# A group norm's inverse roots on four columns, spread by DMA, and one form for all decay differences

## The chip, the cores and the metric

The kernel runs on one core of a Trainium2 chip. The metric is the time of one execution on the device in microseconds. Engines are named TensorE (PE in the profile, its weight loads PEld), VectorE (DVE), ScalarE (ACT), GpSimd (POOL) and SyncE (SP).

## What is computed

One layer of a hybrid decoder: a multi-scale causal pooling branch and a Mamba-2 branch, merged by gates, and then an MLP. 16 meta tokens stand ahead of 512 tokens of width 1024. The change touches the Mamba-2 branch alone. Cut to what matters:

```python
xbc = silu(causal_depthwise_conv(xbc, conv_w, conv_b))          # x, B, C of 8 groups with 4 heads each
a_cs = cumsum(dt * a)                                           # per head, in chunks of 128 tokens
diff = a_cs[:, :, :, None] - a_cs[:, :, None, :]                # decay differences
lmat = exp(where(mask, diff, -inf))
y_diag = einsum("bclsg,bclsgr,bcsgrp->bclgrp", cb, lmat, xdt)
y_off  = einsum("bclgn,bcgrpn,bclgr->bclgrp", cf, prev, exp(a_cs))
y = (y_diag + y_off + x * d_skip) * silu(z)
yg = y.reshape(bsz, seqlen, 8, 256)
yg = yg * rsqrt(mean(yg * yg, axis=-1, keepdims=True) + EPS)    # the scan's group norm
y_ssd = (yg.reshape(bsz, seqlen, 2048) * norm_w) @ w_ssd_out
```

## The kernel before

Channels lie on partitions, and the 512 tokens along the free axis. Each matmul in single precision is made of three in a faster format: `block` (L69, L70) loads a 128x1024 block of weights, ScalarE copies it to its high half `whi`, VectorE subtracts to get the low half `wlo`, and TensorE multiplies high by high, high by low and low by high. There are four buffers of `whi` and `wlo` and three of `raw`.

The scan is done for one group of four heads at a time: `ssd(g, cur)`, eight times. It is a generator, and `weave` alternates its steps with those of a second generator that gives TensorE work: `group_proj(g + 1)`, which projects the next group's B, C, x and z (tiles `bt`, `ct`, `xc`, `zt`; products `px` and `pz`), for g = 4 also `out_half` (products `pso`), and for g = 7 `out_part` (products `psp`). For g = 1, 2, 3 and 5 a gate (`pgp`) is projected as well, between the x and the z of the next group. The order in which each engine meets its instructions is then set by a scheduler that reorders them by its own estimates, so that TensorE's row of matmuls changes from one to another group.

The steps of `ssd` that matter here:

- `abc`, four heads by 512 tokens on all 128 partitions, is read from DRAM (`acs_d`) by a DMA of GpSimd, broadcast to the partitions. Two exponentials of it go to `eb` (L372).
- The tile is then turned in place into decay differences. Heads 0 and 1 go through ScalarE: Relu(bias - a), 8 instructions (L377). Heads 2 and 3 go through VectorE: min(a - bias, 0), 8 instructions (L380). The exponential of the first pair has the scale -1 (L382), that of the second pair 1 (L383).
- Transposes of `bt` and `xc` (`ptb`, `ptm`, `ptx`) give `xdt` and `xdd`; `pcb` is the product of B and C, which VectorE masks into `cbm` (L390) and multiplies into `abc` (L403). `pst` are the states of the chunks, carried on in `st` (L399 to L402).
- `po` (from `st`) and `py` (from `abc`) give `yt`, which VectorE finishes (L419 to L423).
- The group norm: the squares of `yt`, summed over the two halves, are split into `qh` and `ql`; a product with a matrix of ones (`png`, L432) puts the sum of each token on every partition. ScalarE takes the root of all 128 partitions by 512 tokens (L435, tile `rs`), VectorE the reciprocal in four pieces of 128 columns (L437) and the scaling of `yt` (L441); the result is split into `yh` on ScalarE (L444) and `yl` on VectorE (L445).

`rs` and `cbm` have the same tag and share one buffer; so have `eb` and `sqg`, the squares.

Of the kernel before, what the change touches and what calls it, by code (L numbers as in the profile page):

```python
# [9 lines left out]
F32 = mybir.dt.float32  # L10
F32R = mybir.dt.float32r
AF = mybir.ActivationFunctionType
ALU = mybir.AluOpType

P = 128
D = 1024
SEQ = 512
# [4 lines left out]
G = 8  # L22
R = 4
# [22 lines left out]
def kernel(ctx: ExitStack, tc, xT, x, w, vec, fnw, out):  # L46
    nc = tc.nc
    act, dve, pe, pool = nc.scalar, nc.vector, nc.tensor, nc.gpsimd
# [3 lines left out]
    dram = ctx.enter_context(tc.tile_pool(name="dram", bufs=1, space=bass.MemoryType.DRAM))  # L52
# [50 lines left out]
    eps = const.tile([P, 1], F32, name="eps")  # L103
# [7 lines left out]
    dtok = const.tile([P, 2, 4, HEADS], F32, name="dtok")  # L111
# [19 lines left out]
    def psum1(name):  # L131
        return psb.tile([P, 512], F32, tag="s", name=name)
# [41 lines left out]
    for k in range(NK):  # L174
        if k == 0:
# [4 lines left out]
                                 op0=ALU.mult, op1=ALU.subtract)  # L180
# [13 lines left out]
    def col_sums(name, qt, n2, tags, bufs=1):  # L194

        qh = n2.tile(list(qt.shape), F32R, tag=tags[0], name=f"qh{name}", bufs=bufs)
        ql = n2.tile(list(qt.shape), F32R, tag=tags[1], name=f"ql{name}", bufs=bufs)
        act.copy(qh, qt)
        dve.tensor_tensor(ql, qt, qh.bitcast(F32), op=ALU.subtract)
        return qh, ql  # L200


    qh, ql = col_sums("n1", q, pre, ("sq", "sq"), 2)
    for i in range(2):
        c = slice(i * HALF, (i + 1) * HALF)
        pn = psum1(f"pn1_{i}")
# [14 lines left out]
    for c in range(4):  # L221
        r = slice(c * H, (c + 1) * H)
# [20 lines left out]
    for c in (slice(0, P), slice(P, W)):  # L243
        n = c.stop - c.start
        dve.tensor_tensor_scan(acs[:, c], ones_f[:, :n], v[:, c], 0.0, op0=ALU.mult, op1=ALU.add)
    acs_d = dram.tile([H, SEQ], F32, name="acs_d")
    for c in range(4):
        nc.gpsimd.dma_start(acs_d[:, c * P : (c + 1) * P], acs[c * H : (c + 1) * H, :P])
    pt = psum1("pt_dt")
# [79 lines left out]
    def ssd(g, cur):  # L329
# [4 lines left out]
        ctok = lambda c: slice(c * P, (c + 1) * P)  # L334
        flat = lambda t: t.rearrange("p r d -> p (r d)")
        abc = gs.tile([P, R, SEQ], F32, tag="abc", name=f"abc{g}")
# [17 lines left out]
        for b in range(2):  # L354
            pt = psum1(f"ptx{g}_{b}")
            for c in range(2):
                for i in range(2):
                    o = c * 256 + i * P
# [14 lines left out]
        dm = abc.rearrange("p r (c l) -> p r c l", c=4)  # L373
        for r in range(R):
            for c in range(4):
                if r < 2:
                    act.activation(dm[:, r, c, :], dm[:, r, c, :], AF.Relu, scale=-1.0,  # L377
                                   bias=dtok[:, 1, c, R * g + r : R * g + r + 1])
                else:
                    dve.tensor_scalar(dm[:, r, c, :], dm[:, r, c, :], dtok[:, 1, c, R * g + r : R * g + r + 1],  # L380
                                      0.0, op0=ALU.subtract, op1=ALU.min)
        act.activation(abc[:, :2], abc[:, :2], AF.Exp, scale=-1.0)  # L382
        act.activation(abc[:, 2:], abc[:, 2:], AF.Exp)  # L383
        yield

        pc = psum1(f"pcb{g}")
# [20 lines left out]
        for i in range(2):  # L407
# [5 lines left out]
            for c in range(4):  # L413
                for j in range(2):
                    r = 2 * i + j
# [6 lines left out]
                                     op0=ALU.mult, op1=ALU.add)  # L422
# [6 lines left out]
        qh, ql = col_sums(f"g{g}", sq[:, 0, :], gs, ("qh", "ql"))  # L429
        yield  # L430
        pn = psum1(f"png{g}")
        pe.matmul(pn, ones_r, qh, start=True, stop=False)  # L432
        pe.matmul(pn, ones_r, ql, start=False, stop=True)
        rs = gs.tile([P, SEQ], F32, tag="cbm", name=f"rs{g}")
        act.activation(rs, pn, AF.Sqrt, bias=eps, scale=1.0 / 256)  # L435
        for c in range(4):
            dve.reciprocal(rs[:, ctok(c)], rs[:, ctok(c)])  # L437
        yield
        for i in range(2):
            y = yt[:, i, :]  # L440
# [34 lines left out]
    gs = gc_stack.enter_context(tc.tile_pool(name="gs", bufs=1, side="left", reuse_waits="tile"))  # L475
# [29 lines left out]
    for g in range(G):  # L505
        nxt = group_tiles(g + 1) if g + 1 < G else None
        fill = [group_proj(g + 1, nxt, GATE_AT.get(g))] if nxt else [out_part()]
        if g == 4:
            fill = [out_half()] + fill
        weave(ssd(g, cur), fill, 2 if g == 4 else 1)  # L510
        cur = nxt
# [75 lines left out]
    for d in range(NK):  # L587
        ps = psum2(f"pup{d}")[:, :SEQ]
        wh, wl = block()
        for n, k in enumerate(ks):  # L590
            c = slice(k * P, (k + 1) * P)
# [35 lines left out]
    for half in range(2):  # L627
# [5 lines left out]
        for kk in range(4):  # L633
            wh, wl = block()
            for k2 in range(2):
                k = 2 * kk + k2
                c = slice(k2 * 512, (k2 + 1) * 512)
# [4 lines left out]
        c = slice(half * 512, (half + 1) * 512)  # L642
        for t in range(4):
            dve.tensor_tensor(ht[:, t, c], ht[:, t, c], pv[t], op=ALU.add)
        for kk in range(4):
            k = 4 * half + kk
            pt = psum1(f"pth{k}")
            for t in range(4):
# [3 lines left out]
                                     op0=ALU.mult, op1=ALU.subtract)  # L652
        for t in range(4):
            j = hp_.tile([P, 512], F32, tag="junk", name=f"junk{half}_{t}", bufs=1)
# [171 lines left out]
    c = NC - 1  # L826
# [5 lines left out]
    for t in range(4):  # L832
        T, st = t // 2, slice((t % 2) * P, (t % 2 + 1) * P)
        n = 0
        for half in range(2):
            parts = [(0, 512)] if half == 0 or t < 3 else [(0, 256), (256, 256)]
            for a, m in parts:
# [4 lines left out]
                for k, seg in ((1, (A11, 3)[T]), (0, (A12, A22)[T])):  # L842
                    wh, wl = wq[k, half]
                    for p in range(2):
                        x0 = p * 512 + a
                        f = i == 0 and not (T == 0 and half == 0)
# [151 lines left out]
```

## Time and profile before

| | us |
|---|---|
| median of 3 runs | 1035.16 (1035.08 to 1035.29) |
| the profiled execution | 1035.26 |
| its span, from the first to the last instruction | 1033.5 |
| TensorE busy | 1019.6 |
| VectorE busy | 714.2 |
| ScalarE busy | 542.3 |
| GpSimd busy | 9.9 |

The granted clock of TensorE was 0.998 over the span. The time of an execution is 1.8 us more than the span, which begins at the first instruction and ends with the last. The scan (`ssd`) lies between about 69 and 485 us of the span; the pooling branch, the output projections and the MLP come after it. In a row of the profile, L437 is line 437 of the kernel before; `out<-in` names the tiles.

### The profile page before, as it was taken

Reading aid. Unit: us, or ns where it says so; the run is one execution under the profiler, and the core shown is the slowest. Engines: PE = TensorE matmul, PEld = TensorE weight load, DVE = VectorE, ACT = ScalarE, POOL = GpSimd, SP = SyncE. Lnnn points to the kernel's source line nnn. Section 1 sums busy time; section 2 is a strip of 40 time slices with the busy share of each in tenths; the row PEclk is TensorE's granted clock in tenths of the full one; section 3 lists DMA queues with packets and bytes.
Section 4 is the critical chain, followed back from the end, with each engine's and each line's share of the span. In section 5 each row is a group of like instructions: output and inputs, shape, how many; then the busy total and the mean of one; then the engine's idle time right before and its main releaser. Section 6 shows DMA issues by size and latency. Waiting matters only on the chain.

```text
span 1033.5 us, 13995 instructions
## 1 busy us (share of the span) xinstructions
PE 1019.6 (99%) x5700; PEld 880.2 (85%) x5700; DVE 714.2 (69%) x932; ACT 542.3 (52%) x706; POOL 9.9 (1%) x24
## 2 busy tenths in 40 slices
PE   7999999999999999999999999999999999999997
PEld 7889988898879898988998888878888888888886
DVE  7978787687636586878664345645686676776866
ACT  7675968586627349573443123344555354454444
POOL 0100000000000000000000000000000000000000
PEclk9999999999999999999999999999999999999999
DMA  6343041414332321413232323533324323334112
GB/s 229 110 140 103 21 164 37 148 47 137 102 112 73 103 101 41 146 59 111 77 107 95 102 81 102 204 126 122 99 82 123 103 81 122 102 102 123 42 41 82
DMA packets 29424, 106.01 MB, mean 103 GB/s; under 512 B 3312, under 2 KB 4272, under 8 KB 28336
## 3 DMA queue, kind: packets, MB, share of 16 engines
q1 hardware_dynamic: 26640, 93.14, 28.8%
q0 software_dynamic: 2000, 11.08, 2.9%
q8 instruction: 45, 0.74, 0.3%
q10 hardware_dynamic: 720, 0.91, 0.3%
q14 instruction: 19, 0.16, 0.0%
HBM read 102.95 MB, written 2.16 MB: 102 GB/s over the span
## 4 chain that ended last, share of the span: by engine, by line
PE 97%; DVE 1%; DMA 1%; ACT 0%; issue 0%; SPq 0%; ACTq 0%
PE px L138 6%; PE px L141 6%; PE px L139 6%; PE pf L86 6%; PE pf L87 6%; PE pf L88 6%; PE alpha L742 3%; PE alpha L743 3%; PE alpha L744 3%; PE pz L139 3%; PE pz L141 3%; PE pz L138 3%; PE py L416 2%; PE pso L86 2%; PE pp L141 2%; PE pp L139 2%
## 5 line engine op out<-in xcount | busy, mean ns | idle before, releaser
L69 ACT CAST whi<-raw 128x1024 fp32r<-128x1024 f32 (+2 forms) x141 | 145.4, 1037 | 274.3 <-PE pf L87 61.3
L70 DVE TENSOR_TENSOR wlo<-raw,whi 128x1024 fp32r<-128x1024 f32 (+2 forms) x141 | 169.8, 1206 | 151.5 <-ACT whi L69 151.5
L138 PE MATMUL px<-uh,whi 128*128 128x264 f32 (+1 forms) x448 | 121.0, 291 | 0.7 <-DVE ct L280 0.7
L139 PE MATMUL px<-ul,whi 128*128 128x264 f32 (+1 forms) x448 | 118.2, 284 | 0.0
L86 PE MATMUL pf<-vh,whi 128*128 128x512 f32 x256 | 99.7, 389 | 1.2 <-DVE vl L651 1.2
L87 PE MATMUL pf<-vl,whi 128*128 128x512 f32 x256 | 99.6, 389 | 0.0
L88 PE MATMUL pf<-vh,wlo 128*128 128x512 f32 x256 | 99.6, 389 | 0.0
L141 PE MATMUL px<-uh,wlo 128*128 128x264 f32 (+1 forms) x448 | 91.5, 285 | 0.0
L138 PEld LDWEIGHTS px<-uh,whi 128*128 128x128 f32 x448 | 84.6, 189 | 2.8 <-issue 2.6
L139 PEld LDWEIGHTS px<-ul,whi 128*128 128x128 f32 x448 | 84.4, 188 | 0.3
L141 PEld LDWEIGHTS px<-uh,wlo 128*128 128x128 f32 x448 | 69.4, 188 | 0.3 <-issue 0.3
L693 DVE TENSOR_TENSOR slo<-b,shi 128x1024 fp32r<-128x1024 f32 x35 | 42.7, 1220 | 31.6 <-ACT shi L692 31.6
L692 ACT CAST shi<-b 128x1024 fp32r<-128x1024 f32 x35 | 36.7, 1050 | 51.9 <-PE pf L87 36.5
L86 PEld LDWEIGHTS pf<-vh,whi 128*128 128x128 f32 x256 | 48.1, 188 | 11.5 <-DVE vl L651 1.5
L88 PEld LDWEIGHTS pf<-vh,wlo 128*128 128x128 f32 x256 | 48.0, 188 | 10.0
L87 PEld LDWEIGHTS pf<-vl,whi 128*128 128x128 f32 x256 | 48.1, 188 | 9.8
L742 PE MATMUL alpha<-shi,hh 128*128 128x512 f32 x140 | 54.6, 390 | 0.0
L743 PE MATMUL alpha<-slo,hh 128*128 128x512 f32 x140 | 54.5, 389 | 0.0
L744 PE MATMUL alpha<-shi,hl 128*128 128x512 f32 x140 | 54.5, 389 | 0.0
L754 DVE TENSOR_TENSOR ht<-ht,alpha 128x1024 f32<-128x1024 f32 x35 | 42.6, 1216 | 6.1 <-PE alpha L744 6.1
L139 PE MATMUL pz<-ul,whi 128*128 128x512 f32 x112 | 44.3, 395 | 0.0
L141 PE MATMUL pz<-uh,wlo 128*128 128x512 f32 x112 | 44.1, 394 | 0.0
(330 smaller groups left out, 2395.8 us busy)
## 6 DMA issues: line engine op xcount, KB each, us to landing
raw<-in_w SPq DMA_DIRECT2D x137, 512.0 KB, 3.6
b<-in_w SPq DMA_DIRECT2D x28, 512.0 KB, 3.5
abc<-acs_d POOLq DMA_DIRECT2D x8, 1024.0 KB, 7.2
xt<-in_xT SPq DMA_DIRECT2D x8, 264.0 KB, 6.2
ht<-in_x POOLq DMA_DIRECT2D x4, 512.0 KB, 5.0
w<-in_w SPq DMA_DIRECT2D x4, 512.0 KB, 3.5
out_dram<-out SPq DMA_DIRECT2D x4, 320.0 KB, 2.4
raw<-in_w SPq DMA_DIRECT2D x2, 384.0 KB, 5.5
```

What stands on the lines that cost most here:

```text
L69: act.copy(hi[:, c], raw[:, c])
L70: dve.tensor_tensor(lo[:, c], raw[:, c], hi[:, c].bitcast(F32), op=ALU.subtract)
L86: pe.matmul(ps, ah, bh, start=first, stop=False)
L87: pe.matmul(ps, ah, bl, start=False, stop=False)
L88: pe.matmul(ps, al, bh, start=False, stop=last)
L138: pe.matmul(o, wh, rhs[0][k][:, c], start=k == 0, stop=False)
L139: pe.matmul(o, wh, rhs[1][k][:, c], start=False, stop=False)
L141: pe.matmul(o, wl, rhs[0][k][:, c], start=False, stop=k == NK - 1)
L693: dve.tensor_tensor(lo, src, hi.bitcast(F32), op=ALU.subtract)
L742: pe.matmul(ps[t], a[0], wh[:, cs], start=f, stop=False, skip_group_check=True)
L743: pe.matmul(ps[t], a[0], wl[:, cs], start=False, stop=False, skip_group_check=True)
L744: pe.matmul(ps[t], a[1], wh[:, cs], start=False, stop=l, skip_group_check=True)
```

## The change

Two things are changed in `ssd`.

The root of the group norm is taken on one partition only: ScalarE reads the first partition of `png` and writes a row of 512 values. A DMA of GpSimd spreads this row over 128 partitions with four tokens on each (`rc`), VectorE takes the reciprocal of these 128x4 values, a second DMA writes them to a new tensor in DRAM (`rs_d`), and a third reads the 512 values back into all 128 partitions of `rs`. The scaling of `yt` reads `rs` as before.

The decay differences of all four heads go through ScalarE in the Relu form, 16 instructions, and one exponential with the scale -1 takes the whole tile of 128x2048.

```diff
@@ -244,6 +244,7 @@
     acs_d = dram.tile([H, SEQ], F32, name="acs_d")
+    rs_d = dram.tile([G, SEQ], F32, name="rs_d")
@@ -373,14 +374,9 @@
         dm = abc.rearrange("p r (c l) -> p r c l", c=4)
         for r in range(R):
             for c in range(4):
-                if r < 2:
-                    act.activation(dm[:, r, c, :], dm[:, r, c, :], AF.Relu, scale=-1.0,
-                                   bias=dtok[:, 1, c, R * g + r : R * g + r + 1])
-                else:
-                    dve.tensor_scalar(dm[:, r, c, :], dm[:, r, c, :], dtok[:, 1, c, R * g + r : R * g + r + 1],
-                                      0.0, op0=ALU.subtract, op1=ALU.min)
-        act.activation(abc[:, :2], abc[:, :2], AF.Exp, scale=-1.0)
-        act.activation(abc[:, 2:], abc[:, 2:], AF.Exp)
+                act.activation(dm[:, r, c, :], dm[:, r, c, :], AF.Relu, scale=-1.0,
+                               bias=dtok[:, 1, c, R * g + r : R * g + r + 1])
+        act.activation(abc, abc, AF.Exp, scale=-1.0)
         yield
@@ -431,10 +427,15 @@
         pn = psum1(f"png{g}")
         pe.matmul(pn, ones_r, qh, start=True, stop=False)
         pe.matmul(pn, ones_r, ql, start=False, stop=True)
+
+        row = gs.tile([1, SEQ], F32, tag="qh", name=f"row{g}")
+        act.activation(row, pn[:1, :], AF.Sqrt, bias=eps[:1], scale=1.0 / 256)
+        rc = gs.tile([P, 4], F32, tag="rc", name=f"rc{g}", bufs=2)
+        nc.gpsimd.dma_start(rc, row)
+        dve.reciprocal(rc, rc)
+        nc.gpsimd.dma_start(rs_d[g : g + 1, :].rearrange("o (p j) -> (o p) j", j=4), rc)
         rs = gs.tile([P, SEQ], F32, tag="cbm", name=f"rs{g}")
-        act.activation(rs, pn, AF.Sqrt, bias=eps, scale=1.0 / 256)
-        for c in range(4):
-            dve.reciprocal(rs[:, ctok(c)], rs[:, ctok(c)])
+        nc.gpsimd.dma_start(rs, rs_d[g, :].partition_broadcast(P))
         yield
```

## The prediction

> **What bounds the kernel now.** I read the page first: the span, the busy shares, the chain that ended last.
>
> ```profile
> span 1033.5 us, 13995 instructions
> PE 1019.6 (99%) x5700; PEld 880.2 (85%) x5700; DVE 714.2 (69%) x932; ACT 542.3 (52%) x706; POOL 9.9 (1%) x24
> ...
> PE 97%; DVE 1%; DMA 1%; ACT 0%; issue 0%; SPq 0%; ACTq 0%
> ```
>
> TensorE is busy for 1019.6 of 1033.5 us and is 97% of the chain. No matmul is added or removed by the change. So the time that VectorE is spared is worth only what TensorE waits for it now. The view of waits, for TensorE alone, lists all of that:
>
> ```profile
> PE pdt L138 <- ACT xh L178: 5.5, 2, 5.2
> PE pf L86 <- DVE vl L651: 1.2, 1, 1.2
> PE px L138 <- DVE ct L280: 0.7, 1, 0.7
> PE pdt L139 <- DVE xl L179: 0.6, 1, 0.6
> ```
>
> The columns are total us, times and longest. The first and last stand at the start of the kernel and the second behind the output projection; only the 0.7 us on `ct` lie in the scan, where the change is. That is the whole possible gain. The loss has no such bound: every microsecond that TensorE waits in the scan is added to the end, because no later wait is long enough to absorb it.
>
> **What is removed and added on the engines.** The groups of instructions by line:
>
> ```profile
> L437 DVE RECIPROCAL rs<-rs 128x128 f32<-128x128 f32 x32 | 27.2, 911 | 20.7 <-ACT rs L435 20.7
> L377 ACT ACTIVATE abc<-abc,dtok 128x128 f32<-128x128 f32 x64 | 19.8, 389 | 0.2
> L380 DVE TENSOR_SCALAR abc<-abc,dtok 128x128 f32<-128x128 f32 x64 | 14.1, 273 | 8.9 <-ACT eb L372 8.9
> L728 ACT CAST hh<-s 128x2048 fp32r<-128x2048 f32 x7 | 13.4, 1910 | 10.6 <-DVE s L726 10.6
> L382 ACT ACTIVATE abc<-abc 128x1024 f32<-128x1024 f32 x8 | 8.5, 1058 | 0.0
> L383 ACT ACTIVATE abc<-abc 128x1024 f32<-128x1024 f32 x8 | 8.4, 1050 | 2.0 <-DVE abc L380 1.9
> L435 ACT ACTIVATE rs<-png,eps 128x512 f32<-128x512 f32 x8 | 5.5, 689 | 0.1
> ```
>
> For each of the eight groups of heads VectorE loses four reciprocals (27.2/8 = 3.4 us) and eight subtractions (14.1/8 = 1.8 us), 5.2 us together. It gets one reciprocal of 128x4. That one is not in the trace; a 128x128 takes 0.9 us for 128 columns, so four columns lie between nothing and the 0.27 us of a small subtraction, and I take 0.1.
>
> ScalarE gets eight more Relu (19.8/8 = 2.5 us by their union) and one exponential over 2048 columns instead of two over 1024. The 2048-column cast of L728 took 1.9 us against 1.06 + 1.05, so 0.2 us less. The root runs on one partition but over the same 512 columns: I leave it at 0.69 us. ScalarE thus gains 2.3 us of work for each group, at 52% busy.
>
> The reciprocal roots now pass through three DMAs issued by GpSimd, one after another: the row of 512 values is spread to 128 partitions, the four values of each are written to DRAM after the reciprocal, and the 2 KB are read back by all 128 partitions (256 KB). None is in the trace. The nearest rows are in the view of DMA issues (KB of each, us from issue to landing) and in GpSimd's timeline:
>
> ```profile
> ht<-in_x POOLq DMA_DIRECT2D x4, 512.0 KB, 5.0
> out_dram<-out ACTq DMA_DIRECT2D x4, 192.0 KB, 2.6
> raw<-in_w SPq DMA_DIRECT2D x2, 128.0 KB, 2.8
> acs_d<-dacs POOLq DMA_DIRECT2D x4, 16.0 KB, 1.7
> ```
>
> ```profile
> 45.90 2.12 POOL L248 DMA_DIRECT2D acs_d<-dacs  x4 [44.29 <-DVE dacs L245]
> 49.73 0.56 POOL L337 DMA_DIRECT2D abc<-acs_d  x1 [1.70 <-DMA acs_d<-dacs]
> ```
>
> Issuing one costs GpSimd 2.12/4 = 0.53 us; a 16 KB one lands 1.7 us later, and the next, which waited for it, began exactly 1.70 us after. So each of the two 2 KB steps is 0.53 + 1.7 = 2.2 us. The 256 KB read lies between 2.6 us (192 KB) and 5.0 us (512 KB): 2.6 + 64/320 x 2.4 = 3.1, with issue 3.6. Sum with the reciprocal: 2.2 + 0.1 + 2.2 + 3.6 = 8.1 us. These are pieces of 16 bytes, 128 to a transfer, and the weight stream uses the same engines, so I add 0.5: **x = 8.6 us** from the end of the root to the spread tile, where the old path took 3.4 us. The lower bound takes 2.6 us for the read and nothing extra: 7.6. The upper takes 5.0 us for it and, for each small one, the 2.8 us of the 128 KB weight piece: 0.53 x 3 + 2.8 x 2 + 0.1 + 5.0 = 12.3.
>
> [...]
>
> **What waits for x.** The scaling of `yt` (L441, VectorE) now waits for the third DMA. In the built program it stands in one queue with what the next group needs: behind it on VectorE are the split of `yt`, `cbm` (which shares its buffer with the spread tile), the mask product into `abc` (L403) that `py` reads, the state updates that `po` reads, and often a convolution or the low half of a weight block. On ScalarE the casts `yh` wait for it, ahead of the remaining Relu, the exponential and the copy of the first state. On GpSimd only the load of `abc` for the group after next stands behind the three DMAs; it must wait for `py` anyway, so it costs nothing. SyncE's queue is untouched.
>
> Group 6 is the tightest, because the output product `psp` of the last stage wants its `yh` at once:
>
> ```profile
> 446.30 0.69 ACT L435 ACTIVATE rs<-png,eps 128x512 f32<-128x512 f32 x1
> 447.40 1.86 ACT L377 ACTIVATE abc<-abc,dtok 128x128 f32<-128x128 f32 x6
> 449.28 1.28 ACT L383 ACT_TABLE_LOAD   x1
> 452.09 1.28 ACT L444 CAST yh<-yt 128x512 fp32r<-128x512 f32 x2 [0.46 <-DVE yt L441]
> 454.24 0.35 ACT L399 COPY st<-pst 128x256 f32<-128x256 f32 x1
> ...
> 445.97 0.40 DVE L365 TENSOR_TENSOR xddm<-xdtm,decm 16x256 f32<-16x256 f32 x1
> 447.01 0.96 DVE L366 TENSOR_TENSOR xdd<-xdt,dec 128x768 f32<-128x768 f32 x1
> 447.89 3.38 DVE L437 RECIPROCAL rs<-rs 128x128 f32<-128x128 f32 x4
> ...
> 444.08 0.49 PE L345 MATMUL ptb<-ident,bt 128*128 128x128 f32 x3
> 451.28 0.58 PE L86 MATMUL psp<-yh,whi 128*128 128x512 f32 x1
> 451.70 0.39 PE L87 MATMUL psp<-yl,whi 128*128 128x512 f32 x1
> 451.93 0.39 PE L88 MATMUL psp<-yh,wlo 128*128 128x512 f32 x1
> 456.92 0.39 PE L410 MATMUL po<-ct,st 128*128 128x128 f32 x2
> ```
>
> Columns: start, duration, engine. In the new order ScalarE does, from 447.40, sixteen Relu at 1.86/6 = 0.31 (to 452.4), a state copy (0.3), the table load (1.28), the exponential (1.9, to 455.8), and only then the two `yh`, at 0.64 each: the first is there at 456.4, where it was at 452.7. TensorE has twelve `psp` without it, from 451.28 on, at 0.23 and one at 0.42 (starts above), and three `po` at about 0.2: it asks for `yh` at 454.9. So it waits 1.5 us, even if the DMAs cost nothing; with 0.1 for `psp` buffers that VectorE frees later, 1.6. The DMAs add to that when the scaling (0.75 us for the first half) would not be done at 455.8: at x over 455.8 - 0.75 - 446.99 = 8.1 us, one for one.
>
> In groups 2, 3 and 5 the root ends before the transposes of the next group (`ptb`):
>
> ```profile
> 207.18 0.69 ACT L435 ACTIVATE rs<-png,eps 128x512 f32<-128x512 f32 x1
> 212.49 0.49 PE L345 MATMUL ptb<-ident,bt 128*128 128x128 f32 x3
> ...
> 254.46 0.69 ACT L435 ACTIVATE rs<-png,eps 128x512 f32<-128x512 f32 x1
> 261.69 0.49 PE L345 MATMUL ptb<-ident,bt 128*128 128x128 f32 x3
> ...
> 393.35 0.69 ACT L435 ACTIVATE rs<-png,eps 128x512 f32<-128x512 f32 x1
> 400.39 0.49 PE L345 MATMUL ptb<-ident,bt 128*128 128x128 f32 x3
> ```
>
> VectorE's work on the transposes ends 447.89 - 444.08 = 3.8 us after `ptb`. In group 2 the scaling stands behind all of it: it is reached at 212.49 + 3.8 = 216.3, 8.4 us after the root's end at 207.87. In group 3 it stands ahead of `xdd` (0.9): 9.4 us. In group 5 also ahead of `xddm` (0.4): 9.0 us. Beyond that VectorE stands still, and I give group 2 no slack, groups 3 and 5 0.3 us (what the state updates have over before `po`). Group 0's scaling stands behind a convolution as well, group 1's ahead of an exponential that ends later still, and behind groups 4 and 7 nobody waits for `yh`: I cost them at nothing.
>
> **The sum.** The 0.7 us on `ct` stand in group 1, where two `px` blocks are interleaved, the second ahead of the buffer it needs. In the new order they are one behind the other there, so the wait goes; but group 3 now has that interleaving, and I add 0.7 there (bounds: nothing, and twice that). Runs of full-precision matmuls among the others are 53 instead of 54; one such change costs 0.42 - 0.23 = 0.2 us at 451.28: less 0.1. So the change is worth, in us: 1.6 - 0.1 + (x - 8.1) + (x - 8.4) + (x - 9.3) + (x - 9.7), each bracket only where positive. At x = 8.6 it is 1.5 + 0.5 + 0.2 = **+2.2 us**. The profiled execution took 1035.26 us (1033.5 span and 1.8 around it), 0.1 above the median of 1035.16: so 1037.4 us. At x = 12.3 it is 1.5 + 4.2 + 3.9 + 3.0 + 2.6 = +15.2, at x = 7.6 it is +1.5.
>
> **Rivals.** *Short chain*, x at 7.6 to 8.1: only ScalarE's 1.6 us are left, 1035.16 + 1.5 = 1036.7. For it speaks the 1.7 us of the small DMA; against, the 16-byte pieces. Chance 0.18.
>
> *TensorE never waits*, the other side of no change: one place decides, group 6. If `yh` is there before 454.9 instead of 456.4, which needs ScalarE 1.5 us sooner (Relu at 0.2 us each would do), only the 0.7 and 0.1 us are left as a gain: 1034.4; with the wait in group 3, 1035.1. Against it speak the 0.31 us of each Relu and that the casts stand behind the exponential in the built order. Chance 0.15.
>
> *Long chain*, x from 9.6 on: the wait in group 6 is joined by those in 2, 3 and 5. GpSimd issues its DMAs while VectorE is 69% busy; if each of the three issues had to let one VectorE instruction pass (about 0.6 us on average, half of a weight split), x is 10.4 and the change +1.5 + 2.3 + 2.0 + 1.1 + 0.7 = 7.6: 1042.8. Against it: the four issues at 45.90 took 0.53 us each, and the one at 49.73 0.56.
>
> ```profile
> L70 DVE TENSOR_TENSOR wlo<-raw,whi 128x1024 fp32r<-128x1024 f32 (+2 forms) x141 | 169.8, 1206 | 151.5 <-ACT whi L69 151.5
> ```
>
> [...] I give that cause 0.06, and the long chain by whichever cause, slow transfers above all, 0.20.
>
> *It gains*: the 5.2 us of VectorE for each group turn into TensorE time. The waits leave 0.7 us for that; more would have to come out of the matmuls themselves. Chance 0.05.
>
> **How the numbers follow.** My forecast, x between 8.3 and 9.6, gives 1036.9 to 1039.7 and has 0.42; of that 0.35 lies over 0.2% (2.1 us, about what a measurement of this kernel can tell from no change), above 1037.2. Slower: 0.35 + 0.20 = 0.55. Same: 0.07 + 0.18 + 0.15 = 0.40. Faster: 0.05. The range goes from 1035.0, which takes in the short chain and half of the rival without waits, to 1044.0, which leaves out the part of the long chain with x above 10.7.
>
> **What would show it.** The waits of TensorE should list `psp` on `yh` (L86 on L445 of the new file) with 1.5 to 2.5 us, and no `px` on `ct` in group 1. GpSimd's three issues of a group should stand about 2.2 us apart, and the scaling should start 8 to 9 us after the root ends. VectorE's busy time should fall by some 40 us to about 675, ScalarE's rise by some 18 to about 560, TensorE's stay within 2 us. A time at or below 1035.0 with no wait in group 6 would make the step on ScalarE's order wrong; a time above 1040 the length of the chain.

## The result and the profile after

The changed kernel takes 1048.16 us (median of 4 runs, 1047.16 to 1050.17) against 1035.16 before: a ratio of 1.0128, 95% interval 1.011 to 1.0145. It is slower by 13 us, where +2.2 was forecast and 1044.0 was the upper end. The profiled execution took 1048.06 us, with a span of 1046.1. Line numbers from here on are those of the changed kernel, in the view of another run those of that run's kernel: L432 is the root of one row, L434, L436 and L438 are the three DMAs, L435 the reciprocal, L442 the scaling, L445 and L446 the split of `yt`.

The page, its span, busy times and chain:

```profile
span 1046.1 us, 14019 instructions
...
PE 1025.0 (98%) x5700; PEld 882.6 (84%) x5700; DVE 678.1 (65%) x844; ACT 557.2 (53%) x760; POOL 22.9 (2%) x48
...
PE 65%; DMA 1%; DVE 1%; ACT 1%; issue 0%; ACTq 0%; POOLq 0%
```

The chain is followed back only to 334.08 us, the third DMA of group 4, so its shares add up to 68%. VectorE has 36 us less to do and ScalarE 15 more, close to the forecast. TensorE does the same 5700 matmuls, but is busy for 5.4 us more, and 7.2 us of the longer span is idle time. The view of waits, for TensorE and then for VectorE's and GpSimd's new lines (total, times, longest):

```profile
PE pz L138 <- DVE xc L281: 3.5, 2, 2.9
PE psp L86 <- ACT yh L445: 2.2, 1, 2.2
...
PE px L138 <- DVE ct L281: 0.7, 1, 0.7
...
PE png L428 <- ACT qhg L198: 0.5, 1, 0.5
PE po L406 <- DVE st L398: 0.4, 1, 0.4
PE pso L86 <- ACT acc L493: 0.4, 1, 0.4
...
DVE rc L435 <- DMA rc<-row: 37.1, 7, 9.1
...
DVE yt L442 <- DMA rs<-rs_d: 11.0, 5, 4.8
```

The wait of `psp` on `yh` was forecast; the longer one, of `pz` on a convolution of `xc`, was not. The largest of the new lines, 37.1 us of VectorE in front of the reciprocal, will turn out to weigh little.

Where the 12.6 us of span arise, read from the same matmul in both timelines (us):

| start of | before | after | behind by |
|---|---|---|---|
| `ptb` of group 1 | 112.00 | 112.40 | 0.4 |
| `ptb` of group 3 | 212.49 | 213.29 | 0.8 |
| `ptb` of group 4 | 261.69 | 263.97 | 2.3 |
| `ptb` of group 5 | 350.60 | 356.55 | 5.9 |
| `ptb` of group 7 | 444.08 | 450.57 | 6.5 |
| `png` of group 7 | 474.93 | 486.73 | 11.8 |
| first `pup` | 560.78 | 573.29 | 12.5 |

Two stages make most of it: group 4's (+3.7) and group 7's (+5.3), in which the norm of group 6 is finished. Both are in the timeline (start, duration, engine; in brackets the idle time before and what ended it):

```profile
326.94 0.68 ACT L432 ACTIVATE row<-png,eps 1x512 f32<-1x512 f32 x1
...
327.91 0.53 POOL L434 DMA_DIRECT2D rc<-row  x1 [19.64 <-ACT row L432]
330.29 0.54 POOL L436 DMA_DIRECT2D rs_d<-rc  x1 [1.85 <-DVE rc L435]
334.08 0.54 POOL L438 DMA_DIRECT2D rs<-rs_d  x1 [3.25 <-DMA rs_d<-rc]
...
338.84 1.41 DVE L442 SCALAR_TENSOR_TENSOR yt<-yt,vs,rs 128x512 f32<-128x512 f32 x2 [3.74 <-DMA rs<-rs_d]
339.62 0.62 ACT L445 CAST yh<-yt 128x512 fp32r<-128x512 f32 x1 [3.86 <-DVE yt L442]
341.10 0.79 ACT L278 ACTIVATE xc<-px,vs 128x528 f32<-128x528 f32 x1
341.23 1.22 DVE L70 TENSOR_TENSOR wlo<-raw,whi 128x1024 fp32r<-128x1024 f32 x1 [0.26 <-ACT whi L69]
342.37 0.76 DVE L281 SCALAR_TENSOR_TENSOR xc<-px,vs,xc 128x527 f32<-128x527 f32 x1
...
345.35 0.47 PE L138 MATMUL pz<-uh,whi 128*128 128x512 f32 x1 [2.86 <-DVE xc L281]
...
453.53 0.68 ACT L432 ACTIVATE row<-png,eps 1x512 f32<-1x512 f32 x1
...
454.50 0.53 POOL L434 DMA_DIRECT2D rc<-row  x1 [20.56 <-ACT row L432]
456.86 0.54 POOL L436 DMA_DIRECT2D rs_d<-rc  x1 [1.83 <-DVE rc L435]
459.06 0.54 POOL L438 DMA_DIRECT2D rs<-rs_d  x1 [1.67 <-DMA rs_d<-rc]
...
460.97 1.91 ACT L379 ACTIVATE abc<-abc 128x2048 f32<-128x2048 f32 x1
...
462.96 1.41 DVE L442 SCALAR_TENSOR_TENSOR yt<-yt,vs,rs 128x512 f32<-128x512 f32 x2 [0.87 <-DMA rs<-rs_d]
...
464.41 0.80 PE L86 MATMUL psp<-yh,whi 128*128 128x512 f32 x1 [2.24 <-ACT yh L445]
```

In group 4 VectorE stands for 3.7 us in front of the scaling. Nobody needs the scaled `yt` there, but the convolution of the next group's `xc` is queued behind it, and TensorE waits 2.9 us for the buffer that this convolution reads. ScalarE stands as well: it is idle for 3.9 us in front of the first cast `yh`, and the first step of the same convolution (L278, 341.10) comes behind that cast. Before the change the scaling stood ahead of the convolution too, but the root ended at 325.24 and the scaling began 4.1 us later:

```profile
329.32 0.75 DVE L441 SCALAR_TENSOR_TENSOR yt<-yt,vs,rs 128x512 f32<-128x512 f32 x1
...
336.11 2.36 DVE L280 SCALAR_TENSOR_TENSOR xc<-px,vs,xc 128x527 f32<-128x527 f32 x3
```

The chain is longer in group 4 than in group 6: 327.62 (the root's end) to 338.84 is 11.2 us, against 454.21 to 462.96, 8.75 us. The view of DMA, over group 4's stretch, shows the weights moving at the same time and the second and third DMA slower (KB, us from issue to landing):

```profile
raw<-in_w SPq DMA_DIRECT2D x3, 512.0 KB, 3.5
rs<-rs_d POOLq DMA_DIRECT2D x1, 256.0 KB, 4.7
rc<-row POOLq DMA_DIRECT2D x1, 2.0 KB, 1.9
rs_d<-rc POOLq DMA_DIRECT2D x1, 2.0 KB, 3.3
```

In group 6, with no weights on the way, the three DMAs took 1.9, 1.7 and 3.9. Group 7 tells the weights from VectorE's work: its third DMA took 4.6 us with a block of weights moving and VectorE idle throughout, while in groups 0 to 3, 5 and 6 it took 3.6 to 3.9 without weights and with VectorE busy for 1.2 to 2.9 us of it. Behind the wait there something else follows; the windows (length, then busy time of PE, PEld, DVE, ACT and POOL, then the granted clock, DMA share and GB/s):

```profile
462.00:464.00 2.00, 0.17 (x2) 0.00 (x0) 1.13 (x3) 1.14 (x2) 0.00 (x0) 0.95 0.10 25
464.00:466.00 2.00, 1.59 (x5) 1.40 (x6) 2.00 (x5) 1.95 (x4) 0.00 (x0) 0.50 0.00 0
466.00:468.00 2.00, 2.00 (x7) 1.52 (x6) 1.10 (x2) 1.11 (x2) 0.00 (x0) 0.50 0.00 0
468.00:470.00 2.00, 2.00 (x6) 1.61 (x5) 1.77 (x2) 0.85 (x1) 0.00 (x0) 0.50 0.00 0
470.00:472.00 2.00, 2.00 (x9) 1.54 (x9) 2.00 (x3) 0.00 (x0) 0.00 (x0) 0.84 0.00 0
```

From 463.8 to 470.6 us TensorE's clock is half of what it is elsewhere. The products `psp` start 0.43 us apart there and 0.23 apart from 470.8 on. TensorE works at half speed for 6.2 of these 6.8 us, which loses 3.1 us.

**Theories.** The *queue theory*: the loss arises where work that TensorE needs stands in an engine's queue behind an instruction that waits for the DMA chain, in groups 4 and 6; and TensorE's wait is followed by half clock. Its rivals: ScalarE's longer row of Relu and exponential; the transfers themselves; VectorE's standing in front of the reciprocal; a clock that falls for another reason.

### The profile page after: what moved, and what is told of

Its sections match the earlier page's. It is cut to its first block, busy times and chain, and to the rows that moved or that the text cites. A ratio compares the mean times of both kernels' runs of the same rounds, so it can differ in the third digit from the quotient of the medians.

```text
span 1046.1 us, 14019 instructions
## 1 busy us (share of the span) xinstructions
PE 1025.0 (98%) x5700; PEld 882.6 (84%) x5700; DVE 678.1 (65%) x844; ACT 557.2 (53%) x760; POOL 22.9 (2%) x48
## 4 chain that ended last, share of the span: by engine, by line
PE 65%; DMA 1%; DVE 1%; ACT 1%; issue 0%; ACTq 0%; POOLq 0%
PE pf L86 6%; PE pf L87 6%; PE pf L88 6%; PE alpha L743 3%; PE alpha L744 3%; PE alpha L745 3%; PE px L138 2%; PE pp L141 1%; PE pp L139 1%; PE px L141 1%; PE pp L138 1%; PE px L139 1%; PE pgs L139 1%; PE pgs L138 1%; PE pgs L141 1%; PE pw L86 1%
## 5 line engine op out<-in xcount | busy, mean ns | idle before, releaser
L138 PE MATMUL pz<-uh,whi 128*128 128x512 f32 x112 | 44.1, 393 | 3.5 <-DVE xc L281 3.5
```

Of the source, the lines that this page charges most:

```text
L138: pe.matmul(o, wh, rhs[0][k][:, c], start=k == 0, stop=False)
```

## Experiments

**The old norm in group 4, in group 6, in both.** The edit puts the old root and reciprocals back under a condition:

```diff
+        if g in (4,):            # (6,) in the second, (4, 6) in the third
+            rs = gs.tile([P, SEQ], F32, tag="cbm", name=f"rs{g}")
+            act.activation(rs, pn, AF.Sqrt, bias=eps, scale=1.0 / 256)
+            for c in range(4):
+                dve.reciprocal(rs[:, ctok(c)], rs[:, ctok(c)])
+        else:
...
```

> The changed kernel with the old root and reciprocals in group 4 alone; TensorE's order of matmuls stays that of the changed kernel. Queue theory: in group 4 VectorE stands 3.7 us in front of the scaling until the third DMA lands, the convolution of xc stands behind it, and TensorE waits 2.9 us for that convolution (pz). The path from group 4's transposes to group 5's grew by 3.65 us. So the wait of pz on xc goes and the time falls by 3 to 4 us, from 1048.2 to about 1044.5. Rival, ScalarE's longer row of Relu and exponential: nothing that it does is undone, so the time stays within 1 us of 1048.2. Rival, disturbance by the transfers themselves (they share the DMA engines with the weights): one of eight transfers goes, at most 0.5 us.

Measured: 1043.37 us (1042.93 to 1043.92), a ratio of 1.008 (1.0063 to 1.0097). The 2.9 us wait of `pz` is gone; the one that is left is that of group 1:

```profile
PE pz L138 <- DVE xc L281: 0.7, 1, 0.7
```

Group 5's `ptb` starts 2.84 us later than before the change instead of 5.95. Group 4's stage is explained; ScalarE's longer row, unchanged here, is not its cause. The median fell by 4.8 us and not by these 3.1 alone, because in this profile the half clock in group 7's stage lasted 3.4 us instead of 6.8 and that stage was 1.8 us shorter.

> The changed kernel with the old root and reciprocals in group 6 alone. Queue and clock theory: the wait of psp on yh (2.2 us) and that of po on st (0.4 us) go, and with them the 7 us at half clock that follow (3.4 us lost): 1048.2 - 6 = 1042.2, and a granted clock of 0.998 over the span, as before the change. If the dip of the clock has nothing to do with the wait, it stays: 1048.2 - 2.6 = 1045.6 with a clock of 0.996. Rival, ScalarE's longer row alone makes the wait: psp still waits 1.5 us or more on yh and the time stays above 1047.

Measured: 1043.71 us (1041.97 to 1044.82), ratio 1.008 (1.0065 to 1.0095). `psp` no longer waits and there is no half clock there: group 7's `ptb` starts 8.6 us later than before the change and its `png` 7.6, so this stage loses nothing any more. But now the wait of `pz` in group 4, 3.5 us here, comes with 3.4 us of half clock, which it did not in the profiled run of the changed kernel. So the dip is not fixed to a place. The one execution of the four whose granted clock over the span was 0.999 took 1041.97, the 1042.2 that was expected without a dip.

> The changed kernel with the old root and reciprocals in groups 4 and 6. If the two losses are independent they add: 1048.2 - 3.7 - 6 = 1038.5, some 3.3 us above the kernel before (1.5 in the stage of group 3, 0.5 to 1 in groups 1 and 2, 0.7 behind the scan). If one wait merely moves to a later place when another goes, it stays above 1040.

Measured: 1038.62 us (1038.40 to 1038.81), ratio 1.0033 (1.0021 to 1.0045), granted clock 0.998 to 0.999 in all six executions. The two losses add. With the long waits the scatter goes as well: 0.4 us between the runs, 3.0 in the changed kernel.

**Filling the wait.** Products that are there already are repeated while TensorE would wait for `yh`:

```diff
             for c in range(4):
-                pe.matmul(po[:, c * P : (c + 1) * P],
-                          flat(st[c])[:, i * P : (i + 1) * P], ct[:, ctok(c)], start=True, stop=True)
+                for _ in range({1: 8, 2: 6}.get(c, 1) if (g, i) == (7, 0) else 1):
+                    pe.matmul(po[:, c * P : (c + 1) * P],
+                              flat(st[c])[:, i * P : (i + 1) * P], ct[:, ctok(c)], start=True, stop=True)
```

> The changed kernel with thirteen more po products in the last stage, repeats of two that are there already: they fill about 2 us of the time in which TensorE waits for yh, and nothing else is moved. psp starts at the same time (the same yh). Clock theory: TensorE idles less than 1 us there, so its clock is not halved behind the wait: the granted clock is 1.00 from 455 to 480 us and the time falls by about 3.4 us, to 1044.8, although TensorE has more work. Rival, the clock falls for another reason than the wait: half clock for about 7 us remains and the time stays at 1048 or more.

Measured: 1047.18 us (1046.72 to 1047.47), ratio 1.0114 (1.0099 to 1.0129). At the place in question it went as the clock theory said: the wait shrank to 0.42 us, the clock stayed at 1.00, and with `psp` starting 13.85 us after group 7's `ptb` (13.84 in the changed kernel), the stage from that `ptb` to `png` fell from 36.16 to 33.65 us, with more work in it (by the edit twelve products, 7 and 5, and not thirteen). The time missed its forecast, because the wait in group 4, untouched by the edit, now drew the dip. Windows there, of this run:

```profile
345.00:346.00 1.00, 0.78 (x4) 0.67 (x4) 0.07 (x1) 0.83 (x2) 0.00 (x0) 1.00 0.33 131
346.00:347.00 1.00, 1.00 (x4) 0.80 (x3) 0.22 (x1) 1.00 (x2) 0.00 (x0) 0.51 0.00 0
347.00:348.00 1.00, 1.00 (x4) 0.80 (x3) 1.00 (x2) 0.44 (x1) 0.00 (x0) 0.50 0.00 0
348.00:349.00 1.00, 1.00 (x4) 0.71 (x3) 0.96 (x3) 0.00 (x0) 0.00 (x0) 0.50 0.00 0
349.00:350.00 1.00, 1.00 (x5) 0.81 (x4) 0.96 (x2) 0.00 (x0) 0.00 (x0) 0.78 0.81 156
```

Half clock from 346.02 to 349.44, 3.42 us; in the changed kernel it was 6.83, twice that.

**The scaling later in the queue, with the chain as it is.**

```diff
+        sn = gs.tile([P, 2], F32, tag="sn", name=f"sn{g}")
+        if g == 4:
+            dve.scalar_tensor_tensor(sn, nxt[0][:, 0, :2], 0.0, vs[:, V_SN + 2 * g : V_SN + 2 * g + 2],
+                                     op0=ALU.mult, op1=ALU.add)
         for i in range(2):
             y = yt[:, i, :]
-            dve.scalar_tensor_tensor(y, y, col(V_SN, 2 * g + i), rs, op0=ALU.mult, op1=ALU.mult)
+            wn = sn[:, i : i + 1] if g == 4 else col(V_SN, 2 * g + i)
+            dve.scalar_tensor_tensor(y, y, wn, rs, op0=ALU.mult, op1=ALU.mult)
```

> The changed kernel, all three DMAs kept in every group; in group 4 alone the scaling takes its factor from a copy that needs the first half of the next group's xc, so that on VectorE it stands behind that convolution and not ahead of it. TensorE's order is untouched. Queue theory: the chain is as long as before but nobody stands behind it, the wait of pz on xc (2.9 us) goes: 1043.4, as with the old norm in group 4. Rival, the chain itself or its transfers beside the weight stream cost the time: they are all there, so 1047 to 1049.

Measured: 1043.61 us (1042.99 to 1044.27), ratio 1.008 (1.0065 to 1.0095), the same as with the old norm in group 4. Its VectorE timeline:

```profile
339.01 2.36 DVE L281 SCALAR_TENSOR_TENSOR xc<-px,vs,xc 128x527 f32<-128x527 f32 x3
...
342.14 0.16 DVE L442 SCALAR_TENSOR_TENSOR sn<-xc,vs 128x2 f32<-128x2 f32 x1 [0.77 <-ACT xc L283]
342.34 1.42 DVE L447 SCALAR_TENSOR_TENSOR yt<-yt,sn,rs 128x512 f32<-128x512 f32 x2
```

The convolution starts at 339.01, before the third DMA lands at 339.58, and the scaling, 2.8 us behind that landing, holds up nobody. On ScalarE the convolution's first step (337.74) stands ahead of the casts again. So in group 4 the cost was the place in the queue, not the chain and not its transfers: they are all there, and the rival's 1047 to 1049 did not come.

**One half of the change at a time.** First the decay differences alone on ScalarE, with the old norm:

> All decay differences on ScalarE, old norm in all groups. Queue theory (the DMA chain makes the loss): no wait of over 1 us in the scan; 1035 to 1037, the change of the matmuls' order alone costing up to 2 us. Rival, ScalarE's longer row of Relu and exponential makes the loss: psp waits 1.5 us or more on yh in the last stage, and the time is above 1038.

Measured: 1036.96 us (1036.42 to 1038.61, 10 runs), ratio 1.0018 (1.0009 to 1.0027). TensorE waits for nothing new in the scan. This half still costs 1.7 us, and the interval excludes no change: the stage of group 3, from its `ptb` to group 4's, is 1.5 us longer here, as in the changed kernel. In ScalarE's timeline the casts stand ahead of the last two Relu and the exponential:

```profile
451.41 4.20 ACT L376 ACTIVATE abc<-abc,dtok 128x128 f32<-128x128 f32 x14
455.51 1.14 ACT L440 CAST yh<-yt 128x512 fp32r<-128x512 f32 x2
456.55 0.69 ACT L376 ACTIVATE abc<-abc,dtok 128x128 f32<-128x128 f32 x2
```

The longer row by itself makes no wait, in the order that the scheduler sets here, with the casts ahead of the exponential. No run keeps the changed kernel's order, casts behind the exponential, without the DMAs.

Then the norm alone, with the old split of the differences:

> The norm by four-column reciprocals and three DMAs in all groups, the old split of the decay differences. Queue theory: psp still waits about 2 us on yh in the last stage, since the third DMA lands no sooner, and a convolution waits behind the scaling in group 4; 1043 to 1049. Rival, ScalarE's row makes the loss: without the eight more Relu the wait in the last stage goes, 1035 to 1038.

Measured: 1047.46 us (1044.00 to 1051.25), ratio 1.0118 (1.0089 to 1.0146). ScalarE and TensorE at the end of the scan:

```profile
460.88 1.04 ACT L383 ACTIVATE abc<-abc 128x1024 f32<-128x1024 f32 x1
...
465.75 1.28 ACT L450 CAST yh<-yt 128x512 fp32r<-128x512 f32 x2 [1.68 <-DVE yt L447]
...
466.42 0.77 PE L86 MATMUL psp<-yh,whi 128*128 128x512 f32 x2 [2.72 <-ACT yh L450]
```

ScalarE is done with its exponentials at 461.92, 3.8 us before it can start the casts, and `psp` waits all the same: here the DMA chain alone makes the wait. The four executions of this one kernel took 1044.00, 1046.07, 1048.86 and 1051.25 us, at granted clocks of 1.000, 0.997, 0.994 and 0.992: 7 us of scatter go with the clock.

**No reciprocal.**

```diff
-        act.activation(row, pn[:1, :], AF.Sqrt, bias=eps[:1], scale=1.0 / 256)
+        act.activation(row, pn[:1, :], AF.Sqrt, bias=eps[:1], scale=0.0)
...
-        dve.reciprocal(rc, rc)
```

> The changed kernel without the reciprocal of 128x4: the second DMA follows the first at once, the root is taken of a constant, and VectorE no longer stands in front of the reciprocal (37.1 us, the longest new line among the waits). What it leaves out is the norm's values. If VectorE's standing there were the cost, the time would fall by over 5 us to below 1043. Queue theory: what counts is the standing in front of the scaling in two groups, which only starts 0.5 us sooner each; the matmuls' order changes somewhat: 1045 to 1049.

Measured: 1045.92 us (1043.97 to 1048.55), ratio 1.0106 (1.0086 to 1.0127). VectorE's 37.1 us in front of the reciprocal are gone, and the waits of `pz` and `psp` are 2.6 and 1.7 us instead of 2.9 and 2.2. The largest new wait in the list was worth less than a microsecond in TensorE's two long waits; the rest of the 2.2 us, which is within the scatter of both kernels, is not told apart, since the order of the matmuls differs too.

**A longer chain in group 4.**

```diff
+        if g == 4:
+            rs_e = dram.tile([1, SEQ], F32, name="rs_e")
+            nc.gpsimd.dma_start(rs_e, rs_d[g : g + 1, :])
+        nc.gpsimd.dma_start(rs, (rs_e[0, :] if g == 4 else rs_d[g, :]).partition_broadcast(P))
```

> The changed kernel with a fourth DMA in group 4 alone: the 2 KB go from DRAM to DRAM once more before they are spread, so the chain there is about 2.2 us longer. TensorE's order is the same; the scheduler, which takes the chain to be longer, now puts the first of the three steps of the xc convolution ahead of the scaling on VectorE. Queue theory: by the profile of the changed kernel the first step runs while the DMA is under way, the scaling of one half at about 341.1, the two other steps end at about 343.2, and TensorE asks at 342.5: the wait of pz falls from 2.9 to about 1 us, and the time falls to 1044 to 1046.5 in spite of the longer chain. Rival, the length of the chain itself is paid: 2.2 us more, 1050.4 or above.

Measured: 1048.36 us (1046.31 to 1049.93), ratio 1.0119 (1.010 to 1.0139). Neither came true. GpSimd and VectorE:

```profile
333.55 0.52 POOL L440 DMA_DIRECT2D rs_e<-rs_d  x1 [3.05 <-DMA rs_d<-rc]
339.03 0.56 POOL L441 DMA_DIRECT2D rs<-rs_e  x1 [4.95 <-DMA rs_e<-rs_d]
...
338.41 0.76 DVE L281 SCALAR_TENSOR_TENSOR xc<-px,vs,xc 128x527 f32<-128x527 f32 x1
342.70 0.75 DVE L445 SCALAR_TENSOR_TENSOR yt<-yt,vs,rs 128x512 f32<-128x512 f32 x1 [3.53 <-DMA rs<-rs_e]
343.37 0.76 DVE L281 SCALAR_TENSOR_TENSOR xc<-px,vs,xc 128x526 f32<-128x526 f32 x1
```

The step from DRAM to DRAM took 5.5 us from its issue to the next, not 2.2, so that the scaling starts at 342.70 instead of 338.84. Yet TensorE's wait grew from 2.9 to 3.4 us only: one step of the convolution went ahead, and only half of the scaling stands before the next one. 3.9 us more of chain for 0.5 us of wait: the length alone does not set the cost, it matters how much of the needed work is queued behind the wait.

No kernel of these beats the one before.

## Why the prediction was wrong

- *TensorE bounds the kernel, VectorE's 5.2 us a group are worth nothing.* Right: with VectorE at 678.1 and ScalarE at 557.2 us (675 and 560 forecast) nothing was gained anywhere.
- *The length of the chain, x = 8.6 us.* Right in size for six groups (8.75 in group 6), in part by luck. The two small steps came as forecast, 2.2 us from one issue to the next beside the reciprocal (0.18 us, not 0.1). But the view's times to landing are counted from the issue, so adding 0.53 us for the issue of the 256 KB read counted it twice. That and the 0.5 us for small pieces, 1.0 together, stood in for a read that took 3.9 us from issue to landing (3.8 at the median) where 3.1 was taken, and for 0.3 us ahead of the first issue. With weights on the way x was 11.2 in group 4, nearer to the upper bound of 12.3, and 10.4 in group 7. All 24 issues took 0.53 to 0.55 us; VectorE stood still during most of them, but was at work throughout, or nearly, in three (164.92, 334.08, 490.95). The 0.6 us more for each issue, which the rival of a long chain reckoned with, does not show in the length of these three.
- *Group 6, `psp` waits 1.6 us and x - 8.1 more.* 2.2 measured with 8.75: right. ScalarE's exponential and the third DMA ended within 0.1 us of each other (462.88 and 462.96), as the two terms said. That ScalarE's row would cost 1.5 us without the DMAs is not borne out: alone, with the casts ahead of the exponential, it cost no wait.
- *The 0.7 us wait moves from group 1 to group 3.* It did. *Groups 2, 3 and 5* cost next to nothing, as forecast: VectorE stood 0.3 us in front of group 2's scaling and not at all in front of the other two. (Group 5's slack, with the lines shown, comes to 8.8 us and not 9.0, which changes nothing at 8.6.)
- *"Behind groups 4 and 7 nobody waits for `yh`: I cost them at nothing."* **This is the step that failed.** It asked who needs the result and not who stands behind the waiting instruction. The list of what is queued behind the scaling, in the same text, named "often a convolution"; in group 4 that is the convolution that frees `pz`'s buffer. What was put at nothing cost 3.1 to 4.8 us: 5.95 - 2.84 between the same matmul with and without, 1048.16 - 1043.37 in the medians.
- *"Every microsecond that TensorE waits in the scan is added to the end", and no more than that.* The sum took each wait at its own length, and this failed too. A wait in groups 4 or 6 mostly came with half clock; in the profiled run that was 3.1 us behind a wait of 2.2. Without group 6's wait the median is 4.5 us lower, where about 2 was forecast for it.
- *Order of the matmuls: -0.1.* Mis-sized as well: without both long waits the kernel is still 3.3 us slower than before. 1.6 of it are three waits of 0.4 to 0.7 us (`pz` and `png` in group 1, `pso` in group 4); most of the rest is TensorE's busy time, 1022.0 against 1019.6 us. That the other order of `po`, `py` and `px` makes it was not tested.

Together, 4.8 for group 4, 4.5 for group 6 and the 3.3 that are left make 12.6 of the 13.0 us. The direction was right. The rival of a long chain came nearer with its +7.6 us, but by another mechanism: it took an x of 10.4 everywhere and put the rest of the cost into groups 2, 3 and 5, where next to none of it lay.

## What to carry to other kernels

When a step is made longer, list for each place what stands behind it in its engine's queue and which matmul needs that, also where nobody needs the step's own result. The size of a wait in the list says little: without VectorE's 37 us in front of the reciprocal TensorE's two long waits were 0.8 us shorter, while the 3.7 us in front of one scaling cost 3. And where TensorE is the bound, a wait of about two microseconds can cost more than twice its length (2.2 us and 3.1 of lost clock here), and the time scatters with it; a reordering that keeps the transfer and puts other work ahead of the waiting instruction removes it (with the scaling behind the convolution in group 4, 1043.61 us instead of 1048.16).

## What was not expected of the hardware

TensorE's clock fell to 0.50 during or behind 11 of the 13 waits of 1.7 to 3.5 us in the scan that the profiles of the changed kernel and these runs show, and behind none of those under 1 us; the exceptions are the 2.86 us wait of the changed kernel and a 1.74 us one. It stayed there for 3.42 us or for twice that (6.83 in the trace of the changed kernel). The stretches at full clock between two changes are multiples of half of 6.83 as well: 453.97 us in the changed kernel is 133 times 3.413, 573.44 us, behind its dip, 168 times, and 211.6 us between two dips of the norm alone 62 times. On a grid of this step, which is a reading of these lengths, all 13 waits agree: the clock was halved at the end of a step in which TensorE had been idle for 1.87 to 3.10 us in sum, and not where the most was 1.85 us (the 2.86 us wait, cut by the edge at 344.34) or 1.18 (the 1.74 us one). A sharp limit is not shown by that: at the start of the run with the decay differences alone, a step with 1.62 us of idle time was followed by half clock too. The shortest of the 11 waits was 1.76 us (the norm alone, in group 1). What sets the step is not shown.

Small DMAs were slower where weights moved at the same time: 2 KB took 3.3 us to land in group 4, with 0.56 MB moved from 330.2 to 334.0, against 1.7 in group 6, with nothing else on the way. The 2 KB from DRAM to DRAM, in group 4 as well, took 5.5 us from their issue to the next.
